# Token block sums behind the last norm, rope tables behind the stage's end: one change in a two-layer transformer kernel

## The chip, the cores and the metric

The kernel runs on one core of one Trainium2 chip. A core has a matmul engine (PE, with PEld loading its weights), three engines for element-wise work (DVE, ACT, POOL), a queue that issues transfers (SP) and 16 DMA engines. Each engine works through its own list of instructions in order and waits on semaphores where an instruction needs another engine's result. The metric is the device time of one execution in microseconds (us); lower is better.

## The reference

Two layers work on 512 latent tokens and 256 context tokens of width 1024. Every sub-layer is: RMS norm, scale and shift by a conditioning vector, the sub-layer, and a gated residual. Layer 0 has windowed and dense attention heads and a SwiGLU FFN on both streams; layer 1 has differential attention and an FFN on the latents alone. All of it is fp32.

```
for l in range(DEPTH):
    mx = (s_c @ mod_w[l] + mod_b[l])[:, None, :]          # shift, scale, gate: x6
    mc = (s_cc @ mod_w[l] + mod_b[l])[:, None, :]
    hx = _rms(x, norm_mix_w[l]) * (1.0 + scx1) + shx1
    hc = _rms(ctx, norm_mix_w[l]) * (1.0 + scc1) + shc1
    ax, ac = _even_mixer(...) if l % 2 == 0 else _odd_mixer(...)
    x = x + gx1 * ax
    x = x + gx2 * _swiglu(_rms(x, norm_ffn_w[l]) * (1.0 + scx2) + shx2, ffn_w_in[l], ffn_w_out[l])
    if not last:
        ctx = ctx + gc1 * ac
        ctx = ctx + gc2 * _swiglu(_rms(ctx, norm_ffn_w[l]) * (1.0 + scc2) + shc2, ffn_w_in[l], ffn_w_out[l])

def _swiglu(h, w_in, w_out):
    gate, up = jnp.split(h @ w_in, 2, axis=-1)
    return (jax.nn.silu(gate) * up) @ w_out
```

In layer 1 queries and keys are normed per head and rotated: `x0*c - x1*s, x0*s + x1*c` with cosine and sine tables of the token's grid place.

## The kernel before

**Numbers and tiles.** Tokens lie in six tiles of 128: 0 to 3 are latents, 4 and 5 context. An fp32 operand is split into a high part (a cast, on ACT) and a low part (operand minus high part, on DVE or POOL); a product is three matmuls, high by high, high by low and low by high. `hT` holds the normed, transposed latents (high and low), `hTc` the normed, transposed context.

**The norm** (`norm_steps`). For a tile: square and sum on ACT (`nh`), 1/rms on POOL (`rs_n`), scaling on POOL (`nh<-x,rs_n`), eight transposes on PE (`npt`), then per group of four columns the scale and shift, two on DVE and two on ACT (`nhc`), the high part on ACT and the low part on DVE.

**The FFN of layer 0** (`ffn_mixed`) goes over 22 blocks of 128 hidden columns. Blocks 0 and 1 are plain products (`first_half`: `pg` and `pu` from `wg`, `wu`); block 0 does all latents first and then the context, for which both context tiles must be normed. From block 2 on the latents' product is made by blocks, seven products in place of eight, from sums of weight blocks (`Weights.sums1` to `sums4`, on POOL, tile `ws`) and from four sums of token blocks. These are made once in `Terms.make` from the four blocks `b11, b12, b21, b22` of `hT`: f1 and f2 (two rooms of the tag "raw"), f3 and f4 (two of the four rooms of the tag "wr"). All show as `tf` in the profile. `split` and `split_last` cut them into high and low parts: t2 and t1 first, f4 over b12, and t3 later.

**The stage's end.** After block 21 the last down products (`dps`, and the banks `pu`, `pg`) are gated and added to the residual (`residual`: L403 multiplies, L404 adds), tile by tile in the order 4, 5, 0, 1, 2, 3; each finished tile goes into layer 1's first norm. Then come the rope tables (`head_tables`): `rope` is loaded into `rp`, the head gains into `rw`; DVE scales and swaps `rw` and spreads it into `rc`; eight POOL products make the tables `rt`.

**The in-projection of layer 1** (`in_proj1`). Per head four units of weights (256 input rows by 384 columns; below u0 to u3) are loaded by three transfers each into a room of the tag "raw" (`wir`), cast on ACT (`wih`) and subtracted (`wil`): u0 and u2 on POOL, in three pieces, u1 and u3 of heads 0 and 1 on DVE. The tag "raw" has two rooms in all (`raw_tile`); a room is free when the last reader of its tile is done. PE needs `wih` and `wil` of a unit: u0 to u3 on the two context tiles, 12 matmuls of 256 columns each, then on latent tiles 0 and 1.

**What sets the order.** Instructions that are issued through `Pinned` engines (most of `ffn_mixed`) keep the order in which the code is written. All others are placed by a scheduler that simulates the program. `tc.issue_after(i)` keeps what is issued in its scope behind instruction i on that engine; `behind(eng)` is the same with the engine's last instruction so far. Line L764 is the helper that issues all pinned instructions (L763 after the change), so they are told apart by tile names.

## Time and profile before

| | |
|---|---|
| three runs | 1781.36, 1787.05, 1788.74 us |
| median | 1787.05 us |
| profiled execution, its own time | 1785.69 us |
| its span | 1783.9 us |
| mean granted PE clock | 0.985 |
| PE busy, PEld busy | 1679.2 us (94%), 1489.5 us (83%) |
| DVE, ACT, POOL busy | 1195.4 us (67%), 915.3 us (51%), 1053.2 us (59%) |

Times in the profile are counted from the start of the span. PE is busy nearly throughout, so time can be found only where PE stands still or runs at a lower clock; another engine's busy share tells nothing by itself. A row of the timeline gives start, duration, engine, line, operation, written tile, read tiles, and in brackets the idle time ahead of it with what ended it.

### The profile page before, as it was taken

The numbers are of one execution on the slowest core, as the hardware profiler recorded it, in microseconds if no ns is written. First come the engines' busy times: TensorE is split into PE (matmuls) and PEld (weight loads), VectorE is DVE, ScalarE is ACT, GpSimd is POOL, SyncE is SP. The second block draws the span as 40 slices with busy tenths as digits, with TensorE's granted clock in tenths as the row PEclk, the third lists the DMA queues.
The fourth block names the chain that finished last, engine by engine and source line by source line (L and its number), as shares of the span: only waits on it lengthen the run. The fifth ranks groups of instructions, "written<-read, shape, count | busy, mean of one in ns | idle before, by whom it ended". The sixth has DMA issues, their size and how long they took to land.

```text
span 1783.9 us, 30539 instructions
## 1 busy us (share of the span) xinstructions
PE 1679.2 (94%) x11322; PEld 1489.5 (83%) x11322; DVE 1195.4 (67%) x2180; ACT 915.3 (51%) x2030; POOL 1053.2 (59%) x1338
## 2 busy tenths in 40 slices
PE   5999999989799999999999789999998999999998
PEld 3887787767689998899989589999986788999997
DVE  4775555445657767777777746666656388777777
ACT  5556565543335555555553546666665355444441
POOL 1753333423556878788776666666683347777770
PEclk8999999999899999999999889999999999999999
DMA  9212223314243544455543221111132234333332
GB/s 305 64 44 72 83 96 107 119 48 130 69 145 118 154 142 148 149 153 156 154 126 124 91 63 36 37 36 37 37 92 83 81 97 147 94 103 107 107 95 95
DMA packets 206837, 184.80 MB, mean 104 GB/s; under 512 B 17056, under 2 KB 191712, under 8 KB 206688
## 3 DMA queue, kind: packets, MB, share of 16 engines
q1 hardware_dynamic: 206336, 182.65, 33.6%
q8 instruction: 89, 1.46, 0.3%
q14 instruction: 60, 0.49, 0.1%
q10 hardware_dynamic: 352, 0.21, 0.0%
HBM read 173.36 MB, written 9.46 MB: 102 GB/s over the span
## 4 chain that ended last, share of the span: by engine, by line
PE 70%; DVE 8%; POOL 6%; DMA 6%; ACT 5%; issue 3%; SPq 1%; ACTq 0%; POOLq 0%; DVEq 0%
PE dps L764 15%; PE pg L764 10%; PE pu L764 8%; PE cgu L764 5%; PE inps L396 4%; PE inps L397 3%; PE inps L398 3%; DMA modw<-in_mod_w_dram 2%; PE av L547 2%; PE sc L502 2%; POOL wil L286 2%; PE ops L717 2%; PE ops L719 2%; PE ops L718 2%; PE ppt L529 2%
## 5 line engine op out<-in xcount | busy, mean ns | idle before, releaser
L764 POOL TENSOR_TENSOR wbl<-ws,wbh 128x256 fp32r<-128x256 f32 x152 | 122.0, 833 | 124.4 <-PE pu L764 54.1
L764 DVE TENSOR_TENSOR x<-x,dps 128x512 f32<-128x512 f32 x268 | 176.7, 679 | 25.2 <-PE dps L764 25.0
L764 PE MATMUL dps<-wdh,hdh 128*128 128x512 f32 x434 | 174.5, 402 | 10.6 <-DVE x L404 4.4
L764 PE MATMUL pg<-hT,wbh 128*128 128x256 f32 (+1 forms) x944 | 176.2, 284 | 2.5 <-DVE pg L764 1.6
L764 PE MATMUL dps<-wdl,hdh 128*128 128x512 f32 x434 | 172.0, 396 | 0.0
L764 PE MATMUL dps<-wdh,hdl 128*128 128x512 f32 x434 | 171.6, 395 | 0.3 <-DVE hdl L764 0.3
L764 ACT ACTIVATE modw<-modw,cols 128x256 f32<-128x256 f32 x256 | 109.4, 498 | 108.8 <-DMA modw<-in_mod_w_dram 96.5
L764 PEld LDWEIGHTS pg<-hT,wbh 128*128 128x128 f32 x944 | 150.8, 188 | 11.9 <-DVE pg L764 2.0
L764 POOL TENSOR_TENSOR modw<-modw 128x512 f32<-128x512 f32 (+1 forms) x96 | 121.1, 1261 | 63.4 <-ACT modw L764 48.2
L764 POOL TENSOR_TENSOR ws<-wr 128x256 f32<-128x256 f32 x152 | 142.8, 960 | 17.3 <-DMA wr<-in_ffn_w_in_dram 13.6
L396 PE MATMUL inps<-wih,hT 128*128 128x384 f32 x384 | 133.4, 347 | 1.2 <-ACT qkv L594 1.0
L764 PE MATMUL pg<-hT,wbl 128*128 128x256 f32 (+1 forms) x472 | 133.7, 283 | 0.0
L398 PE MATMUL inps<-wih,hT 128*128 128x384 f32 x384 | 131.3, 342 | 0.0
L397 PE MATMUL inps<-wil,hT 128*128 128x384 f32 x384 | 130.9, 341 | 0.0
L764 DVE TENSOR_TENSOR wbl<-wr,wbh 128x512 fp32r<-128x512 f32 x142 | 120.2, 850 | 5.9 <-ACT wbh L764 5.4
L764 PE MATMUL cgu<-hTc,wbh 128*128 128x256 f32 x640 | 114.2, 280 | 0.0
L764 ACT CAST wbh<-ws 128x512 fp32r<-128x512 f32 x152 | 87.4, 624 | 43.8 <-PE pg L764 31.9
L764 ACT CAST wbh<-wr 128x512 fp32r<-128x512 f32 x142 | 87.3, 619 | 39.0 <-PE pg L764 23.1
L764 PEld LDWEIGHTS dps<-wdh,hdh 128*128 128x128 f32 x434 | 81.9, 189 | 25.3 <-DVE x L764 6.9
L764 PEld LDWEIGHTS cgu<-hTc,wbh 128*128 128x128 f32 x640 | 99.9, 188 | 3.4 <-issue 0.4
L764 PEld LDWEIGHTS dps<-wdh,hdl 128*128 128x128 f32 x434 | 81.9, 189 | 20.2 <-DVE hdl L764 0.7
L764 PEld LDWEIGHTS dps<-wdl,hdh 128*128 128x128 f32 x434 | 82.2, 189 | 9.6
(387 smaller groups left out, 5290.7 us busy)
## 6 DMA issues: line engine op xcount, KB each, us to landing
modw<-in_mod_w_dram SPq DMA_DIRECT2D x108, 512.0 KB, 4.4
wr<-in_ffn_w_in_dram SPq DMA_DIRECT2D x84, 512.0 KB, 4.9
wdr<-in_ffn_w_out_dram SPq DMA_DIRECT2D x44, 512.0 KB, 3.6
wir<-in_od_w_in_dram SPq DMA_DIRECT2D x96, 128.0 KB, 2.3
out_dram<-x SPq DMA_DIRECT2D x12, 512.0 KB, 2.6
x<-in_x_dram SPq DMA_DIRECT2D x8, 512.0 KB, 8.7
wir<-in_ev_w_in_dram SPq DMA_DIRECT2D x16, 256.0 KB, 2.8
wor<-in_ev_w_out_dram SPq DMA_DIRECT2D x8, 512.0 KB, 3.6
```

The source lines that it names most:

```text
L286: nc.gpsimd.tensor_sub(lo[c], raw[c], hi[c])
L396: nc.tensor.matmul(ps, hs[0][:, k, :], a, start=k == 0, stop=False)
L397: nc.tensor.matmul(ps, hs[0][:, k, :], b, start=False, stop=False)
L398: nc.tensor.matmul(ps, hs[1][:, k, :], a, start=False, stop=k == KT - 1)
L502: nc.tensor.matmul(sc[:, s0:s0 + c1 - c0], q, kT[:, j, c0:c1], start=j == 0, stop=bool(j and last))
L529: nc.tensor.transpose(pt[:, h, :], Pt[h][:, cs], ident)
L547: mm = nc.tensor.matmul(av[64 * j:64 * j + 64, :], vv[:, vt[kc], :], P4[:, j::2, kc * P:(kc + 1) * P], start=i == 0, stop=i == nk - 1)
L717: nc.tensor.matmul(ps, ohi[:, k, :], a, start=k == first, stop=False)
L718: nc.tensor.matmul(ps, ohi[:, k, :], b, start=False, stop=False)
L719: self.at = nc.tensor.matmul(ps, olo[:, k, :], a, start=False, stop=k == last)
L764: return tc.keep_in_program_order(op(*args, **kw))
```

## The change

1. In `Terms.make` the order of the four sums becomes f1, f2, f4; f1 is issued behind `normed`, the last DVE instruction there was when the last norm had been written, in place of the engine's last instruction at its own place. f4 goes from DVE to POOL.
2. f3 goes from POOL to DVE, and into a step of its own (`make_last`), called after `hidden(0, ...)`.
3. `head_tables` gets its room for `rp` from the caller: the room of the tag "quv" of the FFN's pool, which the last hidden block has left, in place of a room of the tag "raw". Its DVE and POOL instructions are issued behind those engines' last instructions.

```
-    def head_tables(pool, wq, wk, nq, nk, w):
-
-        rp = raw_tile([P, NTX, 2, HD], "rp")
+    def head_tables(pool, wq, wk, nq, nk, w, rp):
+
         nc.sync.dma_start(rp, rope)
...
-    def ffn_mixed(xs, w_down, w_up, fp, turn_over, new_rows, done):
+    def ffn_mixed(xs, w_down, w_up, fp, turn_over, new_rows, done, after):
...
                 f3, f4 = self.f3, self.f4
-                for eng, t, terms in ((pool, f3, ((b22[0], b12[0], sub), (None, b22[1], add), (None, b12[1], sub))),
-                                      (dve, f1, ((b12[0], b11[0], sub), (None, b12[1], add), (None, b11[1], sub))),
+                for eng, t, terms in ((dve, f1, ((b12[0], b11[0], sub), (None, b12[1], add), (None, b11[1], sub))),
                                       (dve, f2, ((b22[0], f1, sub), (None, b22[1], add))),
-                                      (dve, f4, ((b21[0], f2, sub), (None, b21[1], add)))):
-                    for i, (a, b, op) in enumerate(terms):
-                        with behind(eng.eng) if i == 0 and t in (f1, f3) else ExitStack():
+                                      (pool, f4, ((b21[0], f2, sub), (None, b21[1], add)))):
+                    for a, b, op in terms:
+                        with tc.issue_after(after) if t is f1 and a is not None else ExitStack():
                             eng.tensor_tensor(t, t if a is None else f32(a), f32(b), op)
                 self.raws = (f2, f1, f3)
+
+            def make_last(self):
+                for a, b, op in ((b22[0], b12[0], sub), (None, b22[1], add), (None, b12[1], sub)):
+                    dve.tensor_tensor(self.f3, self.f3 if a is None else f32(a), f32(b), op)
...
         end(hidden(0, 0, TOK, *first[0], three()))
+        tt.make_last()
         tt.split(0, 1)
...
     op.close()
+    normed = next(i for i in reversed(nc.cur_bb.bb.instructions) if i.engine == nc.vector.engine)
...
-              lambda t: dram.tile([P, D], F32, name=f"cx{t}", tag=f"cx{t}"), done0)
+              lambda t: dram.tile([P, D], F32, name=f"cx{t}", tag=f"cx{t}"), done0, normed)
...
-    tabs = head_tables(tab.pool, od_qn[0], od_kn[0], 2, 2, fp.pool.tile([P, 2, 2, HD], F32, name="rw", tag="sgc"))
+    with behind(nc.vector), behind(nc.gpsimd):
+        tabs = head_tables(tab.pool, od_qn[0], od_kn[0], 2, 2,
+                           fp.pool.tile([P, 2, 2, HD], F32, name="rw", tag="sgc"),
+                           fp.pool.tile([P, NTX, 2, HD], F32, name="rp", tag="quv"))
```

The scheduler turns this into the following orders.

**DVE at the start of layer 0's FFN.** `tf_5178` is f1, `tf_5179` f2, `tf_4924` f3, `tf_4925` f4; `nhc` and `hTc_4657` belong to the norms of the context tiles. Before:

```order
L300 TENSOR_TENSOR wdl<-wdr,wdh 128x1024
L764 TENSOR_TENSOR tf_5178<-hT_110 128x1024
L271 TENSOR_SCALAR nhc<-npt,aff_108,modc_106 128x128 x2
L764 TENSOR_TENSOR tf_5178<-tf_5178,hT_111 128x1024
L274 TENSOR_TENSOR hTc_4657<-nhc,hTc_4656 128x4x128
L764 TENSOR_TENSOR tf_5178<-tf_5178,hT_111 128x1024
L271 TENSOR_SCALAR nhc<-npt,aff_108,modc_106 128x128
L274 TENSOR_TENSOR hTc_4657<-nhc,hTc_4656 128x4x128
L271 TENSOR_SCALAR nhc<-npt,aff_108,modc_106 128x128
L764 TENSOR_TENSOR tf_5179<-hT_110,tf_5178 128x1024
L271 TENSOR_SCALAR nhc<-npt,aff_108,modc_106 128x128 x2
L764 TENSOR_TENSOR tf_5179<-tf_5179,hT_111 128x1024
```

With the change:

```order
L300 TENSOR_TENSOR wdl<-wdr,wdh 128x1024
L271 TENSOR_SCALAR nhc<-npt,aff_108,modc_106 128x128 x2
L274 TENSOR_TENSOR hTc_4657<-nhc,hTc_4656 128x4x128 x2
L271 TENSOR_SCALAR nhc<-npt,aff_108,modc_106 128x128 x4
L274 TENSOR_TENSOR hTc_4657<-nhc,hTc_4656 128x4x128 x2
L763 TENSOR_TENSOR tf_5178<-hT_110 128x1024
L763 TENSOR_TENSOR tf_5178<-tf_5178,hT_111 128x1024 x2
L763 TENSOR_TENSOR tf_5179<-hT_110,tf_5178 128x1024
L763 TENSOR_TENSOR tf_5179<-tf_5179,hT_111 128x1024
L763 TENSOR_TENSOR pu<-quv,pu 128x768
L763 TENSOR_TENSOR hdl<-pu,hdh 128x768
L763 TENSOR_TENSOR tf_4924<-hT_110 128x1024
```

The sums that stood between the steps of the context norms now stand behind all of them, and f3 (its first row is the last here) stands behind the first hidden block.

**DVE at the stage's end.** `hdl` is the low part of the last hidden block, which the last down products of the latents read. Before:

```order
L764 TENSOR_TENSOR pu<-quv,pu 128x512
L333 TENSOR_SCALAR rw<-rw 128x64
L335 COPY rw<-rw 128x64 x2
L764 TENSOR_TENSOR hdl<-pu,hdh 128x512
L403 TENSOR_TENSOR dps<-dps,g_11014 128x512 x2
L404 TENSOR_TENSOR x_4682<-x_4682,dps 128x512
```

With the change `rw` stands 41 rows behind `hdl`, behind the norm of latent tile 1 and the low part of u3 (`wil`):

```order
L271 TENSOR_SCALAR nhc<-npt,aff_109,modc_107 128x128 x4
L300 TENSOR_TENSOR wil<-wir,wih 128x768
L274 TENSOR_TENSOR hT_111<-nhc,hT_110 128x4x128 x2
L332 TENSOR_SCALAR rw<-rw 128x64
L334 COPY rw<-rw 128x64
L338 COPY rc<-rw 128x128
```

**POOL at the start of layer 1.** `o_11555` and `o_11609` are the scaled tiles 2 and 3. Before, `o_11555`, then u0's `wil` and then the eight tables stand in a row; the end of the tables and what follows (`wil` six times: u2, and u0 of head 1):

```order
L343 TENSOR_TENSOR rt_11666<-rp,rw 128x2x128
L343 TENSOR_TENSOR rt_11667<-rp,rw 128x2x128
L165 TENSOR_SCALAR rs_n<-nss 128x1
L166 TENSOR_TENSOR rs_n<-rs_n,neghalf 128x1
L257 TENSOR_SCALAR o_11609<-x_4549,rs_n 128x1024
L286 TENSOR_TENSOR wil<-wir,wih 128x2x128 x6
L595 COPY vv<-qkv 128x128
```

With the change:

```order
L286 TENSOR_TENSOR wil<-wir,wih 128x2x128 x3
L257 TENSOR_SCALAR o_11555<-x_4380,rs_n 128x1024
L165 TENSOR_SCALAR rs_n<-nss 128x1
L166 TENSOR_TENSOR rs_n<-rs_n,neghalf 128x1
L257 TENSOR_SCALAR o_11609<-x_4549,rs_n 128x1024
L342 TENSOR_TENSOR rt_11666<-rp,rw 128x2x128
L286 TENSOR_TENSOR wil<-wir,wih 128x2x128 x3
L342 TENSOR_TENSOR rt_11666<-rp,rw 128x2x128
```

u0's low part now stands ahead of `o_11555`; the first of the eight tables stands ahead of u2's low part (the second `wil`), and the other seven behind it. On ACT the casts `wih` of u0 and u1 now stand together ahead of the square of tile 2, the cast of u2 ahead of tile 1's scale and shift, the cast of u3 behind it; on SP the six transfers of u0 and u1 stand ahead of the stores of the finished tiles.

## The prediction

> **What bounds the kernel now.** I read the page first: the span, and PE's row of the 40 slices (44.6 us each).

> ```profile
> span 1783.9 us, 30539 instructions
> ...
> PE   5999999989799999999999789999998999999998
> ```

> PE is at nine tenths almost everywhere, so this kernel is as long as PE's work plus PE's holes. Away from its ends the row has three weak slices: the one from 446 us, where layer 0's FFN starts, and the two from 981 us, where that FFN ends and layer 1 begins. The change touches these two places. PE's waits, asked for 425 to 500 us (first row) and 975 to 1070 us (second), name the two holes that end in DVE's work (total, times, longest):

> ```profile
> PE pg L1288 <- ACT hTc L273: 11.8, 1, 11.8
> ...
> PE dps L764 <- DVE x L404: 4.4, 1, 4.4
> ```

> **First place: the token sums (parts 1 and 2).** The timeline of DVE, POOL, ACT and PE:

> ```profile
> 439.19 1.23 DVE L300 TENSOR_TENSOR wdl<-wdr,wdh 128x1024 fp32r<-128x1024 f32 x1 [1.56 <-ACT wdh L299]
> 446.21 3.35 DVE L764 TENSOR_TENSOR tf<-tf,hT 128x1024 f32<-128x1024 f32 x1
> 442.43 3.30 POOL L764 TENSOR_TENSOR tf<-hT 128x1024 f32<-128x1024 f32 x1
> 455.03 1.13 ACT L273 CAST hTc<-nhc 128x512 fp32r<-128x512 f32 x2
> 455.69 0.58 PE L1288 MATMUL pg<-hTc,wgh 128*128 128x256 f32 x1 [11.84 <-ACT hTc L273]
> ```

> PE stands from 443.85 (455.69 less 11.84), when the transposes of the last context tile (5) are done, until ACT casts that tile's first group. ACT is not busy; it waits for DVE's share of the norm, and DVE is in the token sums. They are long as well: while POOL makes f3, a sum takes 3.35 us that as long a subtraction (`wdl`) does in 1.23. A norm with DVE to itself shows what is left when the sums stand behind it:

> ```profile
> 414.63 1.76 DVE L271 TENSOR_SCALAR nhc<-npt,aff,modc 128x128 f32<-128x128 f32 x4
> 417.42 1.29 DVE L274 TENSOR_TENSOR hT<-nhc,hT 128x512 fp32r<-128x512 f32 x2 [1.03 <-ACT hT L273]
> ```

> In the new order DVE leaves `wdl` at 440.4. Tile 4's second half follows: two scalings (half of 1.76: 0.9), ACT's scalings and casts beside them, and the two low parts (1.29), to about 443.5. Then come tile 5's four scalings; PE needs their first cast, which ends 0.6 before the first low part could follow the second cast (417.42 less 0.6, 2.2 to 2.8 us after 414.63; I take 2.8). PE restarts at 446.3 instead of 455.69: **9.4 us gained**. Its bounds are 8 (each of the steps from `wdl` on a few tenths slower) and 11.8 (no hole at all).

> What is late next? Three things have cover:

> ```profile
> 463.77 0.96 DVE L764 TENSOR_TENSOR pu<-quv,pu 128x768 f32<-128x768 f32 x1 [2.41 <-PE pu L1288]
> 460.24 2.41 POOL L764 TENSOR_TENSOR ws<-wr,ws 128x256 f32<-128x256 f32 x2
> 483.00 1.66 ACT L764 CAST wbh<-ws 128x512 fp32r<-128x512 f32 x3
> 477.27 1.23 DVE L764 TENSOR_TENSOR hT<-tf,hT 128x1024 fp32r<-128x1024 f32 x1 [8.30 <-issue]
> ```

> - f1 and f2 are five DVE operations of some 1.2 us with POOL idle: 447.9 (446.3 and the low parts) to 454. The first hidden block's product on DVE, at 463.77, would come at 454.4. Cost nothing; without that fit, tenths.
> - f4 on POOL starts when f2 is done, at 454, and takes twice 2.4 to 3.3 us (the span of f3's row above at most): to 459 or 461. Queued behind it are block 2's weight sums, four pairs like the one above, which ended at 462.65; at 2.4 a pair they now end at 469 to 471. ACT casts them at 483.0, moved up by 9.4 to 473.6. Cost nothing; the cover is some 3 us, and a microsecond beyond it is one of PE's.
> - f3 on DVE is three operations of 1.2 to 3.35 us in an idle stretch of 8.30. At 1.2 it costs nothing; at 3.35 it would push the next step by 2 us. I take nothing, since POOL's weight sums are short pieces.

> **Second place, start: `rw` leaves the way of the last hidden block.** The rows, and two rows of the chain that ended last:

> ```profile
> 983.91 2.35 POOL L764 TENSOR_TENSOR x<-x,xr 128x1024 f32<-128x1024 f32 x1
> 981.01 0.59 ACT L764 CAST hdh<-pu 128x512 fp32r<-128x512 f32 x1 [0.76 <-DVE pu L764]
> 981.92 1.97 DVE L333 TENSOR_SCALAR rw<-rw 128x64 f32<-128x64 f32 x1 [0.94 <-DMA rw<-in_od_qn_dram]
> 983.80 2.50 DVE L335 COPY rw<-rw 128x64 f32<-128x64 f32 x2
> 986.22 0.68 DVE L764 TENSOR_TENSOR hdl<-pu,hdh 128x512 fp32r<-128x512 f32 x1
> ...
> 988.75 5.85 PE dps L764 x18
> 995.47 4.19 PE dps L764 x18
> ```

> Three operations of 64 columns hold DVE for 4.3 us; the last ends with POOL's operation at 986.3. Without them `hdl` starts when ACT's cast is done, at 981.6 instead of 986.22, the bank is free at 984.1 instead of 988.7, and PE, which stopped at 984.39, doesn't stop: 4.4 us. The 18 products after the hole took 5.85 us, as many later 4.19: 1.7 more. **6.0 us**, bounds 4.4 and 6.0. The operations on the way read a PSUM bank each, and the row of `hdl` has the same 0.68 as others of its size, so POOL shouldn't hold them up.

> **Second place, the weights of layer 1's first head.** The rooms of the tag "raw" are the matter:

> ```profile
> 981.48 0.33 SPq L329 DMA_DIRECT2D rp<-in_rope_dram  x1
> 1012.87 0.39 SPq L292 DMA_DIRECT2D wir<-in_od_w_in_dram  x1
> 1019.78 0.38 SPq L292 DMA_DIRECT2D wir<-in_od_w_in_dram  x1
> 1009.15 1.13 POOL L257 TENSOR_SCALAR o<-x,rs_n 128x1024 f32<-128x1024 f32 x1
> 1010.23 2.61 POOL L286 TENSOR_TENSOR wil<-wir,wih 128x256 fp32r<-128x256 f32 x3
> 1012.80 6.95 POOL L343 TENSOR_TENSOR rt<-rp,rw 128x256 f32<-128x256 f32 x8
> 1031.71 2.22 POOL L286 TENSOR_TENSOR wil<-wir,wih 128x256 fp32r<-128x256 f32 x3 [4.23 <-ACT wih L299]
> 1027.54 0.58 PE L397 MATMUL inps<-wil,hTc 128*128 128x256 f32 x1 [2.09 <-POOL wil L286]
> ```

> `rp` holds one of two rooms from 981.48 until the tables are made at 1019.75, so u1 is loaded only when u0 is used up (1012.87), and u2 at 1019.78. PE gets u2's low part at 1027.54. With `rp` elsewhere u0 and u1 are both loaded early. But u2 still needs u0's room, and it now meets another queue: on POOL its low part stands behind the first table, that behind `rw` on DVE, that behind u3's low part and tile 1's norm, and this, on ACT, behind u2's cast. The prices of that chain:

> ```profile
> wir<-in_od_w_in_dram SPq DMA_DIRECT2D x96, 128.0 KB, 2.3
> ...
> 1014.30 4.05 DMA wir<-in_od_w_in_dram
> ...
> 1006.25 0.84 ACT L299 CAST wih<-wir 128x768 fp32r<-128x768 f32 x1
> 1014.07 1.75 ACT L269 ACTIVATE nhc<-npt,modc,aff 128x128 f32<-128x128 f32 x4
> 1006.12 1.29 DVE L274 TENSOR_TENSOR hTc<-nhc,hTc 128x512 fp32r<-128x512 f32 x2
> 1019.31 1.26 DVE L300 TENSOR_TENSOR wil<-wir,wih 128x768 fp32r<-128x768 f32 x1 [0.82 <-ACT wih L299]
> L316 DVE TENSOR_SCALAR rw<-rw x2: 186/759/1332, 28.8 to 91.2; 128x64 f32<-128x64 f32 x2
> ```

> All is moved up by 6.0 first. u0's low part stood at 1010.23 on POOL; now u1's cast stands ahead of tile 2's square on ACT (0.84 later), and tile 2's scaling behind it and not ahead (1.1 earlier): it starts at 1004.0 and ends at 1006.6. Three transfers are issued (0.4 each) and land 2.3 to 4.05 later: 1010.1 to 1011.9. Then u2's cast 0.84, tile 1's scalings 1.75, u3's cast 0.84, u3's low part 1.26, two low parts 1.29, `rw` 0.19, one table 0.87 (an eighth of 6.95), u2's low part 2.6: 9.6 together. PE has u2 at 1019.7 to 1021.5, I take 1020.8 (the later landing is the one measured in this place), against 1027.54. So at this point **6.7 us** are gained in all: the 6.0 from the start, and 0.7 for the rooms. Bounds: 4 (3 us more for handovers and for DVE and POOL holding each other up) and 15 (u2 not held by the table at all, below). The hole is only moved: PE has 24 short matmuls on u0 and u1 from 1006.6 on and then waits some 11 us for u2. The other seven tables (6.1) and head 1's u0 (2.2) then end at about 1029 on POOL, where head 1's u0 ended at 1033.9; so the context's head norms behind it come 5 us earlier, and PE asks for them only after 48 latent products.

> **The sum.** 9.4 + 6.7 = 16.1. The profiled execution took 1785.69, the span and 1.8 around it: 1769.6. It lies 1.4 below the median of the runs shown, so the median would give 1771; I take 1769.5. Behind both places PE is at nine tenths until layer 1's FFN, so what it gains stays; the few matmuls that change places there I cost at nothing, by the same row.

> [...] A short hole here:

> ```profile
> 1044.90 0.34 PE L621 MATMUL kpt<-identr,kd 128*128 128x128 f32 x2 [2.08 <-ACT o L269]
> 1047.44 0.52 PE L396 MATMUL inps<-wih,hT 128*128 128x384 f32 x1
> 1050.11 0.34 PE L396 MATMUL inps<-wih,hT 128*128 128x384 f32 x1
> ```

> After 2.08 us of idling the matmuls take 0.52 instead of 0.34 for some 4 us. The hole that stays at the first place is 2.4 us, so I expect the slow stretch behind it as before, and have no term for it. [...]

> **The rivals.**
> - *The weights stream freely* (0.15). Against my chain: u2's low part could come right after its cast, if the table ahead of it is ready early. For it: the rooms are free. Then u2 is there at 1014, 13.5 earlier than before, and with a shorter slow stretch 15 are gained: 1785.7 - 9.4 - 15 = 1761. Against it: the table stands ahead of u2 in POOL's order, and `rw` behind tile 1's norm.
> - *Only the first place pays* (0.13). The chain from u0's room to u2 costs 7 us more than its rows, through transfers that land late behind the stores of finished tiles and through DVE and POOL in each other's way: 1785.7 - 9.4 = 1776.3.
> - *The change doesn't do what it says* at the first place (0.08): tile 5's norm is held elsewhere, or f4 makes the weight sums late by what the norm gains; then 1785.7 - 6.7 = 1779.
> - *Slower* (0.04): the same POOL queue as one mechanism, the first table. If `rw` comes so late on DVE that u2 reaches PE over 16 us after 1020.8, all of the gain is eaten; at 25 us late the time is 1795. For it: four engines take turns in this chain. Against it: every row of it is under 3 us.

> **How the numbers follow.** The forecast has 0.60, with 1766 to 1773 as its own range from the bounds of its terms. The range reaches to the first two rivals: 1760 to 1778. About 0.5% (8.9 us) is what a measurement of this kernel can tell from no change. Forecast and free streaming are faster by more, and most of the third case: 0.83 faster; 0.13 the same, 0.04 slower.

> **What would show it.** Right: PE's first product on `hTc` comes about 2.4 us after the transposes; no wait of `dps` for DVE's L404 behind the last hidden block; `rp` no longer ahead of `wir` in a "raw" room; and a wait of PE of about 11 us for u2's `wil`, with POOL idle ahead of the first `rt`. Wrong: no such wait on POOL (then 1761); PE waiting for `wbh<-ws` or `hdl` after the first dip (then the gain there went into POOL's longer queue); a transfer as the last thing in the second hole.

## The result, and the profile after

The changed kernel takes **1765.09 us** (median of four runs, 1761.23 to 1766.13) against 1786.33 for the kernel before in the same comparison: a ratio of 0.9881, 95% interval 0.9854 to 0.9907. The profiled execution took 1766.13 where that of before took 1785.69: 19.6 us less. The forecast was 1769.5 us, with 16.1 us between the two executions.

The page of the changed kernel, the span and PE's row of the 40 slices:

```profile
span 1764.3 us, 30538 instructions
...
PE   6999999889899999999999889999998999999998
```

The slice at the start of layer 0's FFN (the eleventh, now from 441 us) has gone from seven tenths to eight, and so has the first of the two weak ones at the start of layer 1 (from 970 us). PE's waits in the same windows as before, 425 to 500 us (first row) and 975 to 1070 us (the others; total, times, longest):

```profile
PE pg L1287 <- ACT hTc L273: 2.4, 1, 2.4
...
PE inps L396 <- POOL wil L286: 4.4, 1, 4.4
PE kpt L620 <- ACT o L269: 2.4, 1, 2.4
PE inps L395 <- ACT wih L299: 1.8, 2, 1.6
```

The hole of 11.8 us is one of 2.4. The wait of `dps` for DVE's residual (4.4) is gone from the list, and the wait for u2's low part is 4.4 us where the forecast had about 11. The timeline at the first place (start, duration, engine, line, operation):

```profile
440.60 1.22 DVE L300 TENSOR_TENSOR wdl<-wdr,wdh 128x1024 fp32r<-128x1024 f32 x1 [1.56 <-ACT wdh L299]
445.19 1.78 DVE L271 TENSOR_SCALAR nhc<-npt,aff,modc 128x128 f32<-128x128 f32 x4 [0.37 <-PE npt L264]
448.03 0.38 PE L1287 MATMUL pg<-hTc,wgh 128*128 128x256 f32 x1 [2.44 <-ACT hTc L273]
449.22 1.22 DVE L763 TENSOR_TENSOR tf<-hT 128x1024 f32<-128x1024 f32 x1
455.56 2.40 POOL L763 TENSOR_TENSOR tf<-hT,tf 128x1024 f32<-128x1024 f32 x1 [12.75 <-DVE tf L763]
```

The norm of tile 5 follows at once on DVE, the sums come behind it, and PE starts on `hTc` 2.44 us after its transposes. The timeline at the second place:

```profile
974.19 0.41 SPq L328 DMA_DIRECT2D rp<-in_rope_dram  x1
996.67 1.26 DVE L300 TENSOR_TENSOR wil<-wir,wih 128x768 fp32r<-128x768 f32 x1
997.99 2.44 SPq L292 DMA_DIRECT2D wir<-in_od_w_in_dram  x5
996.37 2.82 POOL L286 TENSOR_TENSOR wil<-wir,wih 128x256 fp32r<-128x256 f32 x3
1001.49 0.81 ACT L299 CAST wih<-wir 128x768 fp32r<-128x768 f32 x1
1002.59 1.12 POOL L257 TENSOR_SCALAR o<-x,rs_n 128x1024 f32<-128x1024 f32 x1
1003.68 0.74 POOL L342 TENSOR_TENSOR rt<-rp,rw 128x256 f32<-128x256 f32 x1
1004.37 2.80 POOL L286 TENSOR_TENSOR wil<-wir,wih 128x256 fp32r<-128x256 f32 x3
1007.23 0.58 PE L396 MATMUL inps<-wil,hTc 128*128 128x256 f32 x1 [4.37 <-POOL wil L286]
1008.25 0.18 DVE L332 TENSOR_SCALAR rw<-rw 128x64 f32<-128x64 f32 x1
1008.51 5.11 POOL L342 TENSOR_TENSOR rt<-rp,rw 128x256 f32<-128x256 f32 x7 [1.33 <-DVE rw L332]
```

Read it in two steps. u2's load starts at 997.99, when DVE has finished u1's low part (996.67 plus 1.26): it goes into u1's room, and POOL's u0 (until 999.2) is the room of u3. And the first table runs at 1003.68, long before `rw` is scaled on DVE (1008.25). So it can only be a table of k that is made from the weight as it was loaded: by the kernel's text all tables of q need the scaling, and two of the four of k need the swapped copy that DVE makes behind it. The next table waits for `rw` (1.33 us in the last row), and it stands behind u2.

**Where the time came from.** All the traces hold 11322 matmuls in nearly the same order, so a stage can be cut at the same matmul by count and its length compared with that stage of before (matmuls 2600 to 2850 for the first place, 6300 to 6480 for the stage's end, 6480 to 6800 for the weights of the first head). Gains in us, worked out from the starts of these matmuls; "sum" is the difference between the profiled executions, and "all the rest" what the three stages leave of it:

| execution | first place | stage end | weights | all the rest | sum | median of the runs | ratio to before, interval |
|---|---|---|---|---|---|---|---|
| forecast | 9.4 | 6.0 | 0.7 | 0 | 16.1 | 1769.5 | |
| changed kernel | 9.5 | 5.4 | 5.9 | -1.2 | 19.6 | 1765.09 | 0.9881 (0.9854 to 0.9907) |
| e1 first place only | 11.1 | -0.3 | 2.1 | -0.2 | 12.7 | 1772.89 | 0.9927 (0.9907 to 0.9947) |
| e2 second place only | -1.2 | 5.3 | 6.6 | -0.4 | 10.3 | 1775.64 | 0.9937 (0.9919 to 0.9954) |
| e3 order without the room | 10.8 | 5.5 | 1.6 | 2.4 | 20.3 | 1765.44 | 0.9884 (0.9865 to 0.9903) |
| e4 room without the order | 9.4 | -1.0 | 4.8 | 0.7 | 13.9 | 1772.15 | 0.9922 (0.9900 to 0.9943) |
| e5 changed kernel again | 11.1 | 5.4 | 6.4 | -1.0 | 21.9 | 1763.45 | 0.9880 (0.9860 to 0.9901) |
| e6 as e3, again | 9.5 | 5.8 | 3.1 | -0.7 | 17.7 | 1767.94 | 0.9905 (0.9884 to 0.9926) |
| e7 u2 on DVE | 11.1 | 5.4 | 6.9 | 1.8 | 25.2 | 1763.67 | 0.9885 (0.9860 to 0.9910) |
| e8 u2 behind a q table | 11.1 | 5.5 | 0.8 | -0.7 | 16.7 | 1767.99 | 0.9903 (0.9877 to 0.9929) |
| e9 f1 free | 5.9 | 5.2 | 6.3 | -0.6 | 16.8 | 1767.87 | 0.9906 (0.9893 to 0.9920) |
| e10 f3 on POOL | 5.3 | 5.3 | 6.5 | -1.7 | 15.4 | 1768.82 | 0.9909 (0.9893 to 0.9924) |
| e11 f4 on DVE | 9.3 | 5.4 | 6.2 | -0.5 | 20.4 | 1764.51 | 0.9886 (0.9872 to 0.9899) |
| e12 u2 on DVE, lps late | 11.1 | 5.2 | 6.5 | -0.3 | 22.5 | 1763.17 | 0.9888 (0.9872 to 0.9903) |

One execution of e8 took 4157.95 us; its median is that of the other three. The first place agrees with the forecast; what is more than forecast is in the weights. Of the 5.9 us there 3.6 are idle time of PE (14.3 us before, 10.7 now), and 2.4 are shorter matmuls: the granted clock is at half speed for 23.9 us of this stage before and for 13.7 now.

### The profile page after: what moved, and what is told of

Read it like the earlier page. It is cut to its first block, busy times and chain, and to the rows that moved or that the text cites. A ratio compares the mean times of both kernels' runs of the same rounds, so it can differ in the third digit from the quotient of the medians.

```text
span 1764.3 us, 30538 instructions
## 1 busy us (share of the span) xinstructions
PE 1678.2 (95%) x11322; PEld 1488.6 (84%) x11322; DVE 1193.2 (68%) x2181; ACT 916.4 (52%) x2030; POOL 1046.9 (59%) x1337
## 4 chain that ended last, share of the span: by engine, by line
PE 72%; POOL 6%; DVE 6%; DMA 4%; ACT 4%; issue 3%; SPq 0%; ACTq 0%; POOLq 0%; DVEq 0%
PE dps L763 15%; PE pg L763 11%; PE pu L763 9%; PE cgu L763 5%; PE inps L395 3%; PE inps L396 3%; PE inps L397 3%; PE av L546 2%; DMA modw<-in_mod_w_dram 2%; PE ops L716 2%; PE ops L718 2%; PE sc L501 2%; PE ops L717 2%; POOL wil L286 2%; PE av L664 2%
## 5 line engine op out<-in xcount | busy, mean ns | idle before, releaser
L763 PEld LDWEIGHTS pg<-hT,wbh 128*128 128x128 f32 x944 | 150.8, 188 | 11.6 <-DVE pg L763 1.8
L396 PE MATMUL inps<-wil,hT 128*128 128x384 f32 x384 | 131.3, 342 | 0.0
L397 PE MATMUL inps<-wih,hT 128*128 128x384 f32 x384 | 131.2, 342 | 0.0
L763 PEld LDWEIGHTS dps<-wdh,hdh 128*128 128x128 f32 x434 | 81.6, 188 | 21.2 <-DVE x L763 7.2
## 6 DMA issues: line engine op xcount, KB each, us to landing
wir<-in_od_w_in_dram SPq DMA_DIRECT2D x96, 128.0 KB, 2.3
```

Source lines behind the costliest of these rows:

```text
L396: nc.tensor.matmul(ps, hs[0][:, k, :], b, start=False, stop=False)
L397: nc.tensor.matmul(ps, hs[1][:, k, :], a, start=False, stop=k == KT - 1)
L763: return tc.keep_in_program_order(op(*args, **kw))
```

## Experiments

The theory: the two places add up, and the weights gave more than forecast because u2 does not stand behind `rw`. Its rivals: the places are linked; the order of `rw` did all of it and the room nothing; the forecast's chain is wrong in other links as well. All kernels compute the whole result. The edits are against the changed kernel unless it is said otherwise.

**e1: the first place alone.**

```diff
-    with behind(nc.vector), behind(nc.gpsimd):
+    if True:
         tabs = head_tables(tab.pool, od_qn[0], od_kn[0], 2, 2,
...
-                           fp.pool.tile([P, NTX, 2, HD], F32, name="rp", tag="quv"))
+                           raw_tile([P, NTX, 2, HD], "rp"))
```

> The changed kernel with the rope tables as before the change (rp in the raw room, their instructions issued freely): only the token sums are changed. Theory A, the two places add up: the first place keeps its 9.5 us and the second gives nothing, 1785.7 - 9.5 = 1776 in the profiled execution, ratio to before 0.9945; PE's hole ahead of the first product on hTc is 2.4 and the hole of dps behind DVE's residual is 4.4 again. Theory B, the places are linked (the earlier start of the FFN is lost again at the stage's end, or the second place's gain needs it): 1785 or 1770.

**e2: the second place alone**: the terms of the kernel before.

```diff
-                for eng, t, terms in ((dve, f1, ...), (dve, f2, ...), (pool, f4, ...)):
+                for eng, t, terms in ((pool, f3, ...), (dve, f1, ...), (dve, f2, ...), (dve, f4, ...)):
...
-                        with tc.issue_after(after) if t is f1 and a is not None else ExitStack():
-                            eng.tensor_tensor(...)
+                        eng.tensor_tensor(...)
...
-        tt.make_last()
```

> The kernel before with the rope tables of the change alone (issued behind the engines' last instruction, rp in another room). Theory A, the places add up: the hole of 11.8 us at the FFN's start stays and the second place gives 5.4 (stage end) + 6.2 (weights of layer 1's first head) = 11.6: 1774, ratio 0.9935. My forecast's own price for this place was 6.7: 1779, ratio 0.9962. In the trace: u2's low part of layer 1's first head reaches PE about 12 us earlier than before by A, 6.7 earlier by the forecast.

One row of PE's waits in each, e1 at the stage's end and e2 at the FFN's start:

```profile
PE dps L763 <- DVE x L403: 4.4, 1, 4.4
```

```profile
PE pg L1287 <- ACT hTc L273: 11.7, 1, 11.7
```

Each kernel has the hole of the place that it leaves as before. e2 gave 10.3 us, near the 11.6 of theory A, and its weights 6.6, not the forecast's 0.7. e1 gave 12.7, three more than expected: 11.1 at the first place instead of 9.5, and 2.1 in the weights' stage, where the edit leaves the kernel as it was before the change. The former is the clock, as e5 shows: a short hole that is only now and then followed by a slow stretch. In the latter the wait for `kpt` is 1.4 us instead of 2.1 and no slow stretch follows it (a clock of 1.00 from 1025 to 1045 us). By the medians e1 and e2 gain 13.7 and 10.9 us, 24.6 together, against 21.2 and 22.2 for both places at once (e5 is the second). Each ratio is known to 3 to 5 us either way, so the places add up as far as these runs can tell.

**e5: the changed kernel once more.** No edit.

> The changed kernel once more, for a closer interval and a second trace: 1765, ratio 0.988. In the stretches that the change doesn't touch the two traces should agree within some 0.3 us if one trace is enough to price a stage; if they differ by microseconds (the slow clock behind the hole of 2.4 us there or not, the first 400 us longer or shorter), a difference of single traces below that is nothing.

The windows view of PE in the changed kernel's first trace (length, PE busy with its matmuls, granted clock, DMA share, GB/s):

```profile
445.00:450.00 5.00, 2.33 (x18) 1.00 0.01 3
450.00:455.00 5.00, 5.00 (x32) 0.66 0.00 0
```

The same windows in e5, whose hole of 2.4 us lies 2.4 us earlier:

```profile
445.00:450.00 5.00, 4.09 (x32) 1.00 0.01 3
450.00:455.00 5.00, 5.00 (x36) 1.00 0.00 0
```

The same program has the same hole of 2.4 us in both traces. In one the clock falls to 0.66 over 5 us, which is half speed for 3.4 us and costs 1.6; in the other it stays up. So 9.5 and 11.1 are one mechanism with two outcomes, and stages of single traces that differ by some 1.6 us are equal. The first trace also lost 1.6 us between 390 and 400 us, in code that was not touched, at a granted clock of 0.83 (1.00 in e5), which is more than its "rest" of -1.2; the -1.0 of e5 lies elsewhere, 1.3 us of it between matmuls 8500 and 10000.

**e3 and e6: the order without the room**, the same kernel twice.

```diff
-                           fp.pool.tile([P, NTX, 2, HD], F32, name="rp", tag="quv"))
+                           raw_tile([P, NTX, 2, HD], "rp"))
```

> The changed kernel with rp back in the raw room; the tables' instructions still stand behind the engines' last ones. If the room is what let the weights come earlier: the 5.4 us of the stage's end stay and the 6.2 of the weights go, 1766 + 6 = 1772, or more, since the tables now also end later than in the kernel before (up to 1778). If the room did nothing and all came from the order of rw: 1766.

> The kernel with rp in the raw room and the new issue order once more, timed beside the changed kernel. By the stages of the first trace the room is worth 4.3 us (the weights' stage gave 1.6 instead of 5.9), and the total was equal only because this execution was 3 us quicker in the first 400 us and had no slow clock at the FFN's start: then 1769, ratio 0.9905. If the total of the first run is right, the room is worth nothing: 1765.

e3 first spoke for the rival: its median, 1765.44, is that of the changed kernel. But its trace gave 1.6 in the weights' stage and was 3.2 us quicker over the first 2400 matmuls, which the edit doesn't touch, so e6 was timed beside e5: its four runs are 1766.35 to 1768.81, those of e5 1762.58 to 1764.06. The room is worth about 4.5 us by the medians and 3.3 to 4.8 by the stages (6.4 less 3.1 and 1.6); the medians of all eight runs of each kernel, with those of e3 and of the first comparison, lie 3.2 apart. The intervals of the two ratios overlap, so the size is known only roughly. e3's 1765.44 stays a low value of a kernel whose eight runs reach from 1765.04 to 1768.81. PE's waits in e6, 975 to 1070 us, and two rows of its timeline:

```profile
PE inps L395 <- ACT wih L299: 6.8, 4, 4.0
PE inps L396 <- POOL wil L286: 3.4, 3, 1.4
PE inps L396 <- DVE wil L300: 1.3, 3, 0.8
```

```profile
975.02 1.40 SPq L292 DMA_DIRECT2D wir<-in_od_w_in_dram  x3
...
997.03 7.81 SPq L292 DMA_DIRECT2D wir<-in_od_w_in_dram  x6
```

With `rp` in one of the two rooms a single unit is loaded early (three transfers at 975.02), and the next waits until u0 is used up (997.03). PE then stands for each unit in turn.

**e4: the room without the order.**

```diff
-    with behind(nc.vector), behind(nc.gpsimd):
+    if True:
```

> The changed kernel with the tables' instructions issued freely; rp stays out of the raw room. rw on DVE stands ahead of the last hidden block's hdl again: PE's hole of 4.4 us and the slow matmuls behind it come back, 5.4 to 6 us. On POOL all eight tables stand ahead of u2's low part, 5.2 us more than the one table of the changed kernel. If both count in full: 1766 + 11 = 1777. If the tables are done while POOL would wait anyway, only the hole counts: 1772.

PE's waits in e4, 975 to 1070 us, and POOL's tables:

```profile
PE inps L396 <- POOL wil L286: 7.3, 2, 6.8
PE dps L763 <- DVE x L403: 4.1, 1, 4.1
```

```profile
1002.41 6.50 POOL L342 TENSOR_TENSOR rt<-rp,rw 128x256 f32<-128x256 f32 x8
```

The hole of the stage's end is back (4.1), and all eight tables stand ahead of u2's low part, for which PE waits 6.8 instead of 4.4. 1772.15 is the milder of the two expected values: the stage's end counts in full (-1.0 instead of 5.4), the tables by 1 to 1.6 us (4.8 instead of 5.9 and 6.4).

**e8: u2 behind a table that needs `rw`**, the queue that the forecast assumed.

```diff
+    q_table = []
+    def behind_table(lo, raw, hi):
+        with tc.issue_after(q_table[0]):
+            by_pieces(lo, raw, hi)
...
-                    nc.gpsimd.tensor_tensor(tb[u][:, :, i, h0:h0 + m], ...)
+                    made = nc.gpsimd.tensor_tensor(tb[u][:, :, i, h0:h0 + m], ...)
+                    if j == 0 and i == 0 and u == 0:
+                        q_table.append(made.ins)
...
-            ws.append(unit(wh, views, [P, 2, 384], 5, "wi", None if h < 2 and u % 2 else by_pieces))
+            ws.append(unit(wh, views, [P, 2, 384], 5, "wi", None if h < 2 and u % 2 else behind_table if h == 0 and u == 2 else by_pieces))
```

> The changed kernel with u2's low part on POOL issued behind the first table that is made from the scaled rw: the queue that the forecast assumed. rw comes from DVE at 1008.3 in the changed kernel, the table takes 0.7, the low part 2.8: by the forecast's chain PE has u2 at about 1012.2 instead of 1007.2, and the time is 1766 + 5 = 1771. If the chain was wrong in more than this one link (u2's own load, the clock), u2 comes elsewhere: before 1010 or behind 1014.

POOL and PE in e8 (this execution reaches the place about 5 us earlier than the changed kernel's first trace):

```profile
1002.52 4.21 POOL L348 TENSOR_TENSOR rt<-rp,rw 128x256 f32<-128x256 f32 x5 [2.85 <-DVE rw L338]
1006.70 0.72 POOL L286 TENSOR_TENSOR wil<-wir,wih 128x256 fp32r<-128x256 f32 x1
...
1008.74 3.46 POOL L286 TENSOR_TENSOR wil<-wir,wih 128x256 fp32r<-128x256 f32 x5
1009.62 0.58 PE L403 MATMUL inps<-wih,hTc 128*128 128x256 f32 x1 [11.48 <-ACT wih L299]
```

PE's hole is 11.5 us, the weights' stage gives 0.8 us, and the time is 1768.0, 2.9 and 4.5 above the two medians of the changed kernel: with u2 behind `rw` the surplus in the weights is gone. How much one table behind `rw` costs is not shown, since the experiment is no pure copy of the forecast's chain: in this order all seven tables that follow the first, and not one, came ahead of u2's last piece (which ends at 1010.1). In the time of the changed kernel PE has u2 at about 1014.5, 2 us behind the expected 1012.2 and past the 1014 that had been named as a sign of a second wrong link. The seven tables are that difference at least in part, so that the hole and the gain come out near the forecast's 11 and 0.7 is partly luck. And the matmul that ends the hole, 0.5 us before, is one of the next head that the scheduler has put there.

**e7 and e12: u2's low part on DVE**, in e12 with the small product for `nlam` later as well (the second piece of the edit).

```diff
-            ws.append(unit(..., None if h < 2 and u % 2 else by_pieces))
+            ws.append(unit(..., None if h < 2 and u % 2 or h == 0 and u == 2 else by_pieces))
```

```diff
-    nlam = neg_lambda(at.pool)
...
     emit(NT)
+    with behind(nc.tensor), behind(nc.vector), behind(nc.scalar):
+        nlam = neg_lambda(at.pool)
```

> The changed kernel with the low part of u2 (layer 1's first head) made on DVE in one piece instead of on POOL in three. In the changed kernel u2's cast is done at 1002.3 and POOL makes a norm (1.1), one table (0.7) and then u2's low part (2.8), while PE waits 4.4 us till 1007.2. If POOL's queue is what holds PE there: DVE has the low part at about 1003.8, PE restarts 3.4 earlier, the hole of about 1 us brings no slow clock (1.6 more): 1766 - 4 = 1761 to 1762, ratio 0.985. If u3 or the norms of the latent tiles are right behind: the hole comes a few matmuls later and the time stays 1765.

> u2's low part on DVE as in the run before, and the small product lps (for nlam), its loads' consumer on DVE and its exp issued behind the first head's projections. With u2 on DVE alone PE had its hole of 4.4 us gone but then stood 1.7 us for lps, 0.9 and 2.6 for the head's transposes, and the time was that of the changed kernel. If lps was the next bound: 1.7 us and some slow clock less, 1761 to 1762, ratio 0.9865. If the chain of the head norms on POOL (tables, then the square roots) is the bound, kpt waits longer instead and the time stays 1764.

PE's waits from 975 to 1070 us, e7 and then e12:

```profile
PE kpt L620 <- ACT o L269: 2.6, 1, 2.6
...
PE lps L563 <- DVE lpr L561: 1.7, 1, 1.7
...
PE kpt L620 <- POOL kd L605: 0.9, 1, 0.9
```

```profile
PE kpt L620 <- POOL kd L605: 3.0, 1, 3.0
PE kpt L620 <- ACT o L269: 2.4, 1, 2.4
```

The hole of 4.4 us is gone in both, and the time is that of the changed kernel (1763.67 and 1763.17 against 1763.45). In e7 PE reaches the small product and the head's transposes earlier and stands there; without the small product (e12) it stands the longer for `kd`, which POOL makes behind the tables and the head's norms, in one stretch without a gap. The other wait, 2.4 to 2.6 us, ends on ACT, in the norm of a latent tile. So emptying one entry of POOL's queue moves the wait; what bounds this place next is not settled by these two runs. No version tried beats the changed kernel clearly.

**e9, e10, e11: the parts of the first place.** e9 lets f1 go anywhere again, e10 puts f3 back on POOL at the start, e11 puts f4 back on DVE; the three edits in this order.

```diff
-                        with tc.issue_after(after) if t is f1 and a is not None else ExitStack():
+                        if True:
```

```diff
+                for eng, t, terms in ((pool, f3, ((b22[0], b12[0], sub), (None, b22[1], add), (None, b12[1], sub))),
...
-        tt.make_last()
```

```diff
-                                      (pool, f4, ((b21[0], f2, sub), (None, b21[1], add)))):
+                                      (dve, f4, ((b21[0], f2, sub), (None, b21[1], add)))):
```

> The changed kernel with f1 not held behind the last norm (f4 stays on POOL, f3 on DVE later). DVE then makes f1 and a part of f2 between the steps of tile 5's norm again, but with POOL idle. If the old hole was made by the order and by the two engines together: three sums of 1.23 stand ahead of the first cast, PE's hole is 2.4 + 3.7 = 6.1 instead of 11.8, and the time is 1764.5 + 4 to 5.5 (with or without the slow clock) = 1769 to 1770. If the order alone made the hole: 11.8 again, 1774.

> The changed kernel with f3 made on POOL at the start again (beside the norm of tile 5 and beside f1 and f2, which stay behind the norm), and not on DVE later. If POOL's sums lengthen what DVE does beside them: the low parts of tiles 4 and 5 and f1, f2 take 2 to 2.7 times as long, PE's hole grows from 2.4 to about 4, and the first hidden block's product comes 1 to 2 later: 1764.5 + 1.5 to 4 = 1766 to 1768.5. If f3's engine is indifferent and only f1's place counts: hole 2.4, 1764.5.

> The changed kernel with f4 on DVE behind f2, as in the kernel before. It is two sums of 1.23 more ahead of the first hidden block's product on DVE, which comes at 458 instead of 456, and POOL starts block 2's weight sums 5 us earlier. If moving f4 to POOL was free because POOL's sums have cover (the forecast), and DVE's have a little: 1764.5 to 1766.5, so f4 gains 0 to 2 by its move. If POOL's weight sums were what PE waits for behind: faster than 1764.

PE's wait at the FFN's start in e9, then in e10:

```profile
PE pg L1287 <- ACT hTc L273: 5.5, 1, 5.5
```

```profile
PE pg L1287 <- ACT hTc L273: 5.8, 1, 5.8
```

DVE's two low parts of tile 4 in e10, and POOL's sums beside them:

```profile
442.69 4.95 DVE L274 TENSOR_TENSOR hTc<-nhc,hTc 128x512 fp32r<-128x512 f32 x2 [1.06 <-ACT hTc L273]
444.42 5.42 POOL L763 TENSOR_TENSOR tf<-tf,hT 128x1024 f32<-128x1024 f32 x2
```

The old hole of 11.8 us had two causes of about one size. With f1 between the norm's steps but without f3 on POOL (e9) 5.5 us are left, with f1 behind the norm but f3 on POOL (e10) 5.8, with both put right 2.4. So each cause by itself costs 3.1 and 3.4 us, and the two together 9.4: 2.9 us arise only where both are at work. e9's hole is 0.6 shorter than expected, its time (1767.87) 1 to 2 lower. e10 missed by more (4 expected): two low parts that take 1.29 us by themselves took 4.95, while POOL made two sums of 2.7 beside them; the time, 1768.82, lies 0.3 above its expected range. e11 is the changed kernel's time, 1764.51: moving f4 to POOL gained nothing and cost nothing.

## Why the prediction was right, and where not

The time lies in the range of 1760 to 1778, which had been stretched to the first two rivals, and the second place's 11.3 us lie inside its bounds of 4 to 15. But 1765.09 is 0.9 us outside the forecast's own range of 1766 to 1773, about halfway between the forecast (1769.5) and the first rival (1761), and one term of the sum is out by 5 us. The wide bounds caught it; the mechanism of that term was wrong.

- **First place, 9.4 forecast.** 9.5 in the profiled execution, with the hole of 2.4 us that had been worked out. The forecast had no term for the slow stretch behind that hole, since it expected it; it comes in some executions and not in others, so the same change gives 9.5 or 11.1, and that the profiled execution agreed to 0.1 us is luck.
- **The covers there** (f1 and f2, f4 on POOL, f3 on DVE) held: PE's waits behind the hole are the 1.2, 1.0 and 0.3 us of before. f3 on DVE did meet POOL's weight sums (2.72 and 3.32 us for its first and its other two operations), and the idle stretch hid it. Beside it block 2's weight sums ended at 472.0, 1 us behind the 469 to 471 forecast, inside the cover.
- **Stage's end, 6.0 forecast.** 5.2 to 5.8 in the executions that have the new order. The hole and the slow stretch are gone as described (in the changed kernel a clock of 1.00 from 975 to 1005 us).
- **Weights, 0.7 forecast, 5.9 measured: this step failed.** The sentence was that on POOL u2's low part "stands behind the first table, that behind `rw` on DVE". The order with the change showed the table ahead of u2, rightly; that this table needs the scaled `rw` was assumed. It is a table of k and needs only the load. e8 put u2 behind a table that does need `rw`, and the gain of this stage fell to 0.8 us behind a hole of 11.5 (with six more tables in the way than the forecast had). A second link was wrong in the same direction and by less: u2's load goes into u1's room, whose low part DVE ends at 997.93, and not into u0's, which POOL ends at 999.19. The size of the term was soft as well: with the later landing, which the text says it takes, its own chain ends at 1021.5 and leaves nothing for the rooms, with the earlier one at 1019.7 and leaves 1.8; the 1020.8 behind the 0.7 lies between them.
- **The first rival, weights that stream freely,** had the mechanism right: u2 reaches PE at 1007.2 here, which is 1015.1 in the time of before (plus the 7.9 us gained up to this stage), against 1014 in the rival and 1020.8 in the forecast. Its price of 15 us was too high, since the hole of 4.4 us is still followed by a slow stretch (a clock of 0.64 and 0.68 from 1005 to 1015), and POOL spends 2 us on a norm and a table between u2's cast and u2's low part.
- **"Only the first place pays" and "the change doesn't do what it says"** fell: e2 has the second place's gain by itself, and the rows above show the first. So did "slower", for which u2 had to come 16 us later than forecast.
- **The slow stretch behind the hole.** The forecast expected it by a single row, the hole of 2.08 us. Of the ten traces with the hole of 2.4 us four show the slow stretch (a clock of 0.66 from 450 to 455 us in the changed kernel's first trace) and six don't (1.00 there in e5), so that row was too little to count on it. Within a trace the clock changes only at multiples of 3.41 us, and where the hole falls between two of them splits the ten traces into the four and the six (last section). By these ten, what looks like chance from one execution to the next is the hole's place in time.

## What to carry to other kernels

When a low part, a table or a load stands behind another in a queue, read for each entry which operand it really waits for, tile by slice: two tables of one name had different inputs, and 5 us hung on it. An operation that is moved behind a stage's end is worth not only the hole it made but what its new place lets others do; price the rooms and the order apart, since here neither alone gave the whole. And before a stage of a single trace is explained to the microsecond, take a second trace of the same program.

## What the runs showed of the hardware

```profile
446.62:450.03 3.41, 1.77 (x12) 1.00 0.02 5
450.03:453.45 3.42, 3.42 (x19) 0.50 0.00 0
453.45:456.86 3.41, 3.41 (x28) 1.00 0.00 0
```

No run moved the hole within a step on purpose, and how much idling in a step brings the clock down is not shown. With every hole of 3.9 us or more at either place it fell to half speed in the kernel before, the changed kernel, e1 to e6 and e8, and at the first place of e9 and e10 (for 10.2 us with the 11.8 of before, for 6.8 with the 4.4 of the changed kernel's first trace). At the later wait for `kpt` it was at half speed where the wait took 2.1 to 2.6 us (3.4 us long from 1046.43 on in the kernel before; also in the changed kernel, e2, e5 and e7), and not at the 1.4 us of e1; a hole of 1.6 us in the changed kernel's first trace, ahead of 1042.4, had a slow stretch too (3.4 us from 1043.92 on).

- **DVE and POOL beside each other.** A DVE subtraction of 128x512 took 0.65 us with POOL idle and 2.5 beside POOL's sums of 2.7 (e10); POOL's pairs of weight sums took 1.4 us with DVE idle (e9) and 2.4 to 3.4 beside it (the kernel before, e10). This looks like whole operations taking turns: in the kernel before, one such DVE subtraction began at 443.46 and ended at 446.28, 0.55 us behind a sum of POOL, and the DVE sum that followed ended at 449.56, 1.08 us behind POOL's next one; by themselves they take 0.65 and 1.2.
